# A hybrid DiT layer: shared scan chunks, lasting bias tables and shared value blocks in the stage of scan and attention

## The chip, the cores and the metric

The kernel runs on one core of a Trainium2 chip. The metric is device time in microseconds for one execution. The kernel before took 1521.46 us, the median of three runs (1518.48 to 1524.15).

The core has a matrix engine (PE, with its weight loads PEld), a vector engine (DVE), a scalar engine (ACT), GpSimd (POOL) and SyncE (SP), each with its own instruction stream that it works off in order, and 16 DMA engines that move data between HBM and the on-chip memories. In this kernel SP issues nearly all transfers, one after the other.

## The reference

One layer of a backbone over 1024 latent tokens and 256 context tokens of width 1024. After adaptive norm and one input projection, the columns split into two groups: a gated DeltaNet (four heads of 128, a scan over the sequence in both directions, the context first) and a neighbourhood attention (eight heads of 64, a window of 8 rows by 16 columns on a grid of 16 by 64, with a learned bias and all context keys in one softmax). Both go through one output projection, then a SwiGLU feed-forward network.

```python
px = modulate(rms_norm(x, norm1_w[i]), sh1, sc1) @ w_in[i]
pc = modulate(rms_norm(ctx, norm1_w[i]), csh1, csc1) @ w_in[i]
dn_c, s_ctx_f, s_ctx_b = gated_deltanet(pc[..., :DN_IN], ..., s_zero, s_zero)
dn_x, _, _ = gated_deltanet(px[..., :DN_IN], ..., s_ctx_f, s_ctx_b)
na_x = neighborhood_attention(qx, kx, vx, kc, vc, na_rpb[i], rows)
x = x + g1 * (jnp.concatenate([dn_x, na_x], axis=-1) @ w_out[i])
x = x + g2 * swiglu(modulate(rms_norm(x, norm2_w[i]), sh2, sc2), w_ffn_in[i], w_ffn_out[i])
...
# neighborhood_attention, for the row block r
s_win = jnp.einsum("bnqhd,binchd->bhnqic", q_r, k_r) + bias
s_win = jnp.where(col_valid[:, :, None, :], s_win, -jnp.inf)
s_ctx = jnp.einsum("bnqhd,bkhd->bhnqk", q_r, k_ctx)
p = jax.nn.softmax(jnp.concatenate([s_win.reshape(...), s_ctx], axis=-1), axis=-1)
o = einsum(p_win, v_r) + einsum(p[..., n_win:], v_ctx)
...
# the scan, for each chunk
v_new = u_i - w_i @ S
o_i = (q_i * exp(gam_i)) @ S + qk_i @ v_new
S = S * exp(g_last) + k_dec.T @ v_new
```

The chunks are a way to compute the scan: the kernel uses chunks of 128 tokens, ten in all, of which the first two are the context.

## The kernel before

The kernel has stages in a row: adaptive-norm modulation, input projection, convolution and the preparation of the chunks, then the stage that the change touches, in which the scan and the attention run beside each other (about 552 to 780 us of the profile), then the output projection w_out (from 780 us) and the feed-forward network to the end. Intermediate results lie in HBM between stages.

**The scan.** The loop at L1306 makes ten steps. In step i the forward direction works on chunk ORDER[0][i] (0, 1, 2, ... 9) and the backward one on ORDER[1][i] (1, 0, 9, 8, ... 2). `load(d, c)` at L269 issues the transfers for direction d and chunk c one step ahead: kT, v, y, kt, and for the latent chunks also qT and at, each 128 x 512 floats (256 KB). kT, kt, v and qT depend on the chunk alone; y and at on the direction too. Each tile has three buffers, except that the first step's tiles (`own`) lie in a pool of their own, `begins`, which is closed at step 1 and makes room for the output accumulator oacc. `scan` (L1186) computes one step of one direction in generator pieces; its state S is a new tile `s0` or `s1` in each step. `finish` (L1246) normalises and gates a chunk that both directions have passed, and writes the operands gah and gal of the output projection.

**The attention.** 32 "pairs" follow one another: four pairs of heads, two halves of the rows (`half`), four blocks of columns (`cb`). `pair` (L322) computes the scores of two heads into PSUM (`sc`), adds the bias table in a DVE instruction that also takes the row maximum (L342, out in bt), takes the exponential on ACT in place (L344), normalises on DVE in place (L346), transposes bt on PE (L104, called from L353), copies to pt on ACT (L355) and multiplies with the values vw and vc. The bias tables are tiles bt of 128 x 640 floats in five buffers, two for each pair: `biases` (L301) clears the 256 context columns on POOL (L305) and loads 128 x 384 (L306, 192 KB) for every pair. There are three cases of column blocks (CASE = 0, 1, 1, 2), so that blocks 1 and 2 have equal tables. `values` (L310) loads three of the four groups of rows of a column block (192 KB) for every pair; the two halves of a block share two of them.

**The order.** `beside(PACE)` (PACE = 0.72) advances the attention by so many pieces for each piece of the scan. From the program so written, a scheduler makes each engine's own order, with priorities by program order; on SP all loads stand in one queue, so that a load which must wait for its buffer holds up all loads behind it.

**Towards w_out.** `two_blocks` (L1279) multiplies the attention's half of the first two w_out blocks during the last step and takes its weight pieces from the scan's buffers. After the stage, w_out's weights are loaded to wraw (L217) and split to whi on ACT (L218) and wlo on DVE (L220); the products with gah and gal follow (sc<-gah,whi). Next to it stand the first loads of the feed-forward network's weights, wq<-w_gu (L1393), split to uhi on ACT (L1421) and ulo on DVE (L1422).

Of the kernel before, what the change touches and what calls it, by code (L numbers as in the profile page):

```python
# [9 lines left out]
F32 = mybir.dt.float32  # L10
# [44 lines left out]
AT = (0, 128)  # L55
CTX = {256: slice(0, 256), 0: slice(384, 640)}
PACE = 0.72
ORDER = [list(range(NCH)), [1, 0] + list(range(9, 1, -1))]

# [30 lines left out]
def hybrid(ctx, tc, a, dbg):  # L90
# [174 lines left out]
    ready = {}  # L265
    begins = ExitStack()

    def load(d, c, own=None):

        kT, kt, y, v = (own.tile([128, 4, 128], F32, name=n, tag=f"{n}{d}") if own else  # L270
                        (scan_v if n == "v" else scan_in).tile([128, 4, 128], F32, name=n, tag=n, bufs=3)
                        for n in ("kT", "kt", "y", "v"))
        sp.dma_start(kT, kT_d[:, :, c * 128:(c + 1) * 128])
        sp.dma_start(fl(v), v_d[c * 128:(c + 1) * 128])
        sp.dma_start(y, y_d[d, c])
        sp.dma_start(fl(kt), k_d[c * 128:(c + 1) * 128])
        qT = at = None
        if c >= 2:
            qT, at = (scan_in.tile([128, 4, 128], F32, name=n, tag=n) for n in ("qT", "at"))
            sp.dma_start(qT, qT_d[:, :, (c - 2) * 128:(c - 1) * 128])  # L280
            sp.dma_start(at, at_d[d, c - 2])
        ready[d, c] = kT, qT, kt, v, y, at
# [5 lines left out]
    def attention(nw):  # L288
# [10 lines left out]

        def biases(hp, half, cb):  # L300

            out = []
            for u, w0 in enumerate(WIN):
                bt = nw.tile([128, 640], F32, name="bt", tag="bt", bufs=5)
                pool.memset(bt[:, CTX[w0]], 0.0)  # L305
                sp.dma_start(bt[:, w0:w0 + 384], a["rpb"][2 * hp + u, half, CASE[cb]])  # L306
                out.append(bt)
            return out

        def values(hp, half, cb):  # L310
            vw = nw.tile([128, 3, 128], F32, name="vw", tag="vw", bufs=3)
            sp.dma_start(vw, vw_d[:, cb, half:half + 3, hp * 128:hp * 128 + 128])
            return vw
# [9 lines left out]
        def pair(heads, bts, vw, vc, half, cb, out):  # L323

            r0 = 4 * half
            mx = nw.tile([128, 2, 4], F32, name="mx", tag="mx", bufs=3)
            for u, (head, w0, bt) in enumerate(zip(heads, WIN, bts)):
# [14 lines left out]
                dve.tensor_tensor_reduce(bt, sc, bt, 1.0, -3.0e38, OP.add, OP.max, m[:, 0:1])  # L342
                dve.tensor_scalar(m[:, 1:2], m[:, 0:1], -1.0, None, op0=OP.mult)
                act.activation(bt, bt, AF.Exp, bias=m[:, 1:2], accum_out=m[:, 2:3])  # L344
# [32 lines left out]
        for n, (hp, half, cb) in enumerate(order):  # L377
            if half == 1 and cb in (0, 2) and hp + 1 < NAH // 2:
                heads.setdefault(hp + 1, []).append(load(2 * hp + 2 + cb // 2))
                if cb == 0:  # L380
                    vcs[hp + 1] = context(hp + 1)
# [1455 lines left out]
```

## Time and profile before

| what | us |
|---|---|
| median of the three timed runs | 1521.46 |
| profiled execution, its own time | 1521.66 |
| its span | 1519.9 |
| PE busy in the span | 1455.5 |
| DVE, ACT, POOL busy | 1010.1, 703.1, 183.3 |
| DMA moved in the whole span | 276.28 MB |

The mean granted clock of PE is 0.990 in this execution. The page gives the busy time of each engine, the span in 40 slices, the DMA queues, the chain of work that ended last and the costliest groups of instructions. In the names `out<-in` of an instruction L100 is the helper that issues matmuls and L104 the one that issues transposes, so the tiles tell which is which: `sc<-cst,bt` is a transpose of the softmax, `sc<-kh,qs` a score, `ps<-vk,kt` a product of the scan. SPq is SP's issue of a transfer. A bracket behind a row of a timeline gives the idle time of the engine before the instruction and what ended it.

The chain of work that ended last doesn't reach back before 706 us in this trace, so the stage is read from its waits and timelines.

### The profile page before, as it was taken

The page shows a single profiled execution, that of the slowest core. Times are in us where ns is not written, and L with a number is a line of the kernel's source. Part 1 is how long each engine was busy: PE and PEld are TensorE (multiplying, and loading weights), DVE is VectorE, ACT ScalarE, POOL GpSimd, SP SyncE. Part 2 cuts the span into 40 slices and gives each one's busy share as a digit, 9 for nine tenths or more (in the row PEclk, how much of TensorE's full clock was granted, in tenths as well). Part 3 has the DMA queues.
Part 4 walks back from the last instruction along what each step waited for, and adds up shares of the span by engine and source line. Part 5 has one row for each costly group of instructions (what it writes and reads, how often), then busy time and mean ns, then how long its engine had stood idle before and what let it go on. Part 6 is the DMA issues. An engine that isn't in the chain of part 4 may idle for free.

```text
span 1519.9 us, 23452 instructions
## 1 busy us (share of the span) xinstructions
PE 1455.5 (96%) x8365; PEld 1208.0 (79%) x8365; DVE 1010.1 (66%) x1908; ACT 703.1 (46%) x1379; POOL 183.3 (12%) x251
## 2 busy tenths in 40 slices
PE   6999998899999998999898999999999999999998
PEld 3789787678877777888787888788888888888887
DVE  4787579455677436779977398766665556699652
ACT  5443461674366545656733284333333334354441
POOL 0154500343134300000100000000000000000000
PEclk9999999999999999999999999999999999999999
DMA  9377133565477798999529415333333335798752
GB/s 368 113 229 238 54 94 122 198 170 176 135 214 251 223 289 239 284 269 274 178 76 322 139 35 183 122 105 103 104 102 101 105 104 172 259 366 284 235 153 83
DMA packets 209829, 276.28 MB, mean 182 GB/s; under 512 B 15968, under 2 KB 116912, under 8 KB 208688
## 3 DMA queue, kind: packets, MB, share of 16 engines
q1 hardware_dynamic: 208992, 274.41, 56.3%
q8 instruction: 66, 1.08, 0.3%
q14 instruction: 51, 0.42, 0.1%
q10 hardware_dynamic: 720, 0.37, 0.1%
HBM read 209.93 MB, written 68.98 MB: 184 GB/s over the span
## 4 chain that ended last, share of the span: by engine, by line
PE 45%; DVE 4%; DMA 2%; ACT 1%; issue 1%; SPq 0%; DVEq 0%; ACTq 0%
PE ps L100 42%; PE sc L100 2%; DMA wad<-wa 1%; PE sc L104 1%; DVE x L1591 1%; DVE ulo L1422 1%; DVE acc L254 0%; DMA wraw<-w_out 0%; DVE x L1567 0%; DVE bt L342 0%; DVE lT L1562 0%; DVE x L1470 0%; ACT x L1571 0%; DVE lB L1575 0%; DMA f_d<-g 0%
## 5 line engine op out<-in xcount | busy, mean ns | idle before, releaser
L100 PE MATMUL ps<-hT,uhi 128*128 128x512 f32 x496 | 146.9, 390 | 1.5 <-DVE e L1712 1.4
L100 PE MATMUL ps<-lT,uhi 128*128 128x512 f32 x496 | 146.5, 390 | 0.0
L100 PE MATMUL ps<-hT,ulo 128*128 128x512 f32 x496 | 146.3, 390 | 0.0
L100 PE MATMUL blk<-hh,whi 128*128 128x512 f32 (+1 forms) x456 | 138.8, 397 | 1.9 <-ACT hh L724 1.5
L100 PE MATMUL blk<-hh,wlo 128*128 128x512 f32 (+1 forms) x456 | 130.0, 378 | 0.0
L100 PE MATMUL ps<-hB,uhi 128*128 128x512 f32 x436 | 129.3, 390 | 0.0
L100 PE MATMUL blk<-hl,whi 128*128 128x512 f32 (+1 forms) x456 | 129.2, 377 | 0.0
L100 PE MATMUL ps<-lB,uhi 128*128 128x512 f32 x436 | 128.9, 390 | 0.0
L100 PE MATMUL ps<-hB,ulo 128*128 128x512 f32 x436 | 128.8, 390 | 0.0
L1421 ACT CAST uhi<-ws 128x512 fp32r<-128x512 f32 x91 | 54.7, 622 | 144.8 <-PE ps L100 81.8
L1421 ACT CAST uhi<-wq 128x512 fp32r<-128x512 f32 x101 | 60.3, 621 | 131.3 <-PE ps L100 70.2
L1422 DVE TENSOR_TENSOR ulo<-wq,uhi 128x512 fp32r<-128x512 f32 x101 | 67.2, 688 | 64.8 <-ACT uhi L1421 35.6
L100 PEld LDWEIGHTS ps<-hT,uhi 128*128 128x128 f32 x496 | 93.0, 188 | 21.3 <-ACT uhi L1421 1.7
L100 PEld LDWEIGHTS ps<-lT,uhi 128*128 128x128 f32 x496 | 93.1, 188 | 19.7 <-DVE lT L1575 0.4
L100 PEld LDWEIGHTS ps<-hT,ulo 128*128 128x128 f32 x496 | 93.2, 188 | 19.3
L100 PEld LDWEIGHTS ps<-hB,uhi 128*128 128x128 f32 x436 | 81.9, 188 | 17.4 <-issue 0.5
L100 PEld LDWEIGHTS ps<-lB,uhi 128*128 128x128 f32 x436 | 81.8, 188 | 17.2 <-DVE lB L1575 0.3
L100 PEld LDWEIGHTS ps<-hB,ulo 128*128 128x128 f32 x436 | 81.9, 188 | 16.9
L100 PEld LDWEIGHTS blk<-hh,wlo 128*128 128x128 f32 x456 | 80.7, 191 | 17.8 <-issue 2.5
L100 PEld LDWEIGHTS blk<-hl,whi 128*128 128x128 f32 x456 | 81.0, 190 | 15.2
L100 PEld LDWEIGHTS blk<-hh,whi 128*128 128x128 f32 x456 | 77.5, 192 | 19.1 <-ACT hh L724 3.2
L1422 DVE TENSOR_TENSOR ulo<-ws,uhi 128x512 fp32r<-128x512 f32 x91 | 60.7, 686 | 36.0 <-ACT uhi L1421 27.9
(337 smaller groups left out, 3051.1 us busy)
## 6 DMA issues: line engine op xcount, KB each, us to landing
wq<-w_fo SPq DMA_DIRECT2D x99, 256.0 KB
wq<-w_gu SPq DMA_DIRECT2D x88, 256.0 KB
wad<-wa SPq DMA_DIRECT2D x64, 256.0 KB
bt<-rpb SPq DMA_DIRECT2D x64, 192.0 KB
t_d<-g SPq DMA_DIRECT2D x22, 512.0 KB
fr<-t_d SPq DMA_DIRECT2D x44, 256.0 KB
f_d<-g SPq DMA_DIRECT2D x33, 256.0 KB
fr<-f_d SPq DMA_DIRECT2D x33, 256.0 KB
```

The lines of the kernel that those rows point to most:

```text
L100: i = nc.tensor.matmul(*args, **kw)
L104: i = nc.tensor.transpose(*args, **kw)
L1421: act.copy(hi, self.raw[key])
L1422: dve.tensor_tensor(lo, self.raw[key], hi.bitcast(F32), OP.subtract)
L1591: dve.tensor_tensor(B[at][:, k], B[x][:, k], B.get(y, B["B11"])[:, k], OP.subtract)
```

## The change

- **Chunks.** TWICE holds the chunks that both directions use in two neighbouring steps, with the roles swapped: 0, 1, 5 and 6. Their kT, v, kt and qT are loaded for the direction that comes first and kept for the other (`chunks`). y and at are loaded as before. The pool of the first step's tiles is now closed at step 2.
- **Tables.** Two lasting sets of two tables are cleared once. A set is loaded only when the pair of heads, the half or the case changes. The order of the pairs within a pair of heads becomes TILES, so that equal tables and equal column blocks follow one another: six loads of a set for eight pairs.
- **Values.** A column block is loaded with all four groups of rows and used for both halves.
- **Softmax.** It is computed in tiles of its own, ex, in four buffers, and not in place in the table.
- **State.** The scan's state is updated in place.
- **Room.** The tile sq has the shape of one head, 128 x 128, and one weight piece of `two_blocks` comes from the buffers of v and not from the attention's pool.

```diff
...
 AT = (0, 128)
+TILES = ((0, 0), (0, 1), (1, 1), (2, 1), (2, 0), (1, 0), (3, 0), (3, 1))
 CTX = {256: slice(0, 256), 0: slice(384, 640)}
...
 ORDER = [list(range(NCH)), [1, 0] + list(range(9, 1, -1))]
+TWICE = {c for i in range(NCH - 1) for c in ORDER[0][i:i + 2] if set(ORDER[0][i:i + 2]) == set(ORDER[1][i:i + 2])}
...
     fl = lambda x: x.rearrange("p a b -> p (a b)")
-    ready = {}
+    ready, chunks = {}, {}
     begins = ExitStack()
...
-        kT, kt, y, v = (own.tile([128, 4, 128], F32, name=n, tag=f"{n}{d}") if own else
-                        (scan_v if n == "v" else scan_in).tile([128, 4, 128], F32, name=n, tag=n, bufs=3)
-                        for n in ("kT", "kt", "y", "v"))
-        sp.dma_start(kT, kT_d[:, :, c * 128:(c + 1) * 128])
-        sp.dma_start(fl(v), v_d[c * 128:(c + 1) * 128])
+        def tile(n):
+            if own:
+                return own.tile([128, 4, 128], F32, name=n, tag=f"{n}{d}")
+            return (scan_v if n == "v" else scan_in).tile([128, 4, 128], F32, name=n, tag=n, bufs=3)
+
+        old = chunks.pop(c, None)
+        kT, qT, kt, v = old or (tile("kT"), tile("qT") if c >= 2 else None, tile("kt"), tile("v"))
+        if not old:
+            sp.dma_start(kT, kT_d[:, :, c * 128:(c + 1) * 128])
+            sp.dma_start(fl(v), v_d[c * 128:(c + 1) * 128])
+        y = tile("y")
         sp.dma_start(y, y_d[d, c])
-        sp.dma_start(fl(kt), k_d[c * 128:(c + 1) * 128])
-        qT = at = None
+        if not old:
+            sp.dma_start(fl(kt), k_d[c * 128:(c + 1) * 128])
+        at = None
         if c >= 2:
-            qT, at = (scan_in.tile([128, 4, 128], F32, name=n, tag=n) for n in ("qT", "at"))
-            sp.dma_start(qT, qT_d[:, :, (c - 2) * 128:(c - 1) * 128])
+            if not old:
+                sp.dma_start(qT, qT_d[:, :, (c - 2) * 128:(c - 1) * 128])
+            at = tile("at")
             sp.dma_start(at, at_d[d, c - 2])
+        if not old and c in TWICE:
+            chunks[c] = kT, qT, kt, v
         ready[d, c] = kT, qT, kt, v, y, at
...
+        lasting_bt = [[nw.tile([128, 640], F32, name=f"bt{u}{i}", tag=f"bt{u}{i}", bufs=1) for u in range(2)]
+                      for i in range(2)]
+        for two in lasting_bt:
+            for w0, bt in zip(WIN, two):
+                pool.memset(bt[:, CTX[w0]], 0.0)
+        tables, blocks = [None, 0], {}
+
         def biases(hp, half, cb):
...
-            out = []
-            for u, w0 in enumerate(WIN):
-                bt = nw.tile([128, 640], F32, name="bt", tag="bt", bufs=5)
-                pool.memset(bt[:, CTX[w0]], 0.0)
-                sp.dma_start(bt[:, w0:w0 + 384], a["rpb"][2 * hp + u, half, CASE[cb]])
-                out.append(bt)
-            return out
+            key = hp, half, CASE[cb]
+            if tables[0] != key:
+                out = lasting_bt[tables[1] % 2]
+                for u, w0 in enumerate(WIN):
+                    sp.dma_start(out[u][:, w0:w0 + 384], a["rpb"][2 * hp + u, half, CASE[cb]])
+                tables[:] = key, tables[1] + 1
+            return lasting_bt[(tables[1] - 1) % 2]
...
         def values(hp, half, cb):
-            vw = nw.tile([128, 3, 128], F32, name="vw", tag="vw", bufs=3)
-            sp.dma_start(vw, vw_d[:, cb, half:half + 3, hp * 128:hp * 128 + 128])
-            return vw
+            if (hp, cb) not in blocks:
+                vw = nw.tile([128, 4, 128], F32, name="vw", tag="vw", bufs=3)
+                sp.dma_start(vw, vw_d[:, cb, :, hp * 128:hp * 128 + 128])
+                blocks[hp, cb] = vw
+            return blocks[hp, cb][:, half:half + 3]
...
-            r0 = 4 * half
+            r0, exs = 4 * half, []
             mx = nw.tile([128, 2, 4], F32, name="mx", tag="mx", bufs=3)
...
                 m = mx[:, u]
-                dve.tensor_tensor_reduce(bt, sc, bt, 1.0, -3.0e38, OP.add, OP.max, m[:, 0:1])
+                ex = nw.tile([128, 640], F32, name="ex", tag="ex", bufs=4)
+                dve.tensor_tensor_reduce(ex, sc, bt, 1.0, -3.0e38, OP.add, OP.max, m[:, 0:1])
                 dve.tensor_scalar(m[:, 1:2], m[:, 0:1], -1.0, None, op0=OP.mult)
-                act.activation(bt, bt, AF.Exp, bias=m[:, 1:2], accum_out=m[:, 2:3])
+                act.activation(ex, ex, AF.Exp, bias=m[:, 1:2], accum_out=m[:, 2:3])
                 dve.reciprocal(m[:, 3:4], m[:, 2:3])
-                dve.tensor_scalar(bt, bt, m[:, 3:4], None, op0=OP.mult)
+                dve.tensor_scalar(ex, ex, m[:, 3:4], None, op0=OP.mult)
+                exs.append(ex)
             yield 1
             pts = []
-            for u, bt in enumerate(bts):
+            for u, ex in enumerate(exs):
                 held = slot()
...
                 for j in range(5):
-                    pe.transpose(sc[:, j * 128:(j + 1) * 128], bt[:, j * 128:(j + 1) * 128], ident)
+                    pe.transpose(sc[:, j * 128:(j + 1) * 128], ex[:, j * 128:(j + 1) * 128], ident)
                 pt = nw.tile([128, 640], F32, name="pt", tag="pt", bufs=3)
...
-        order = [(hp, half, cb) for hp in range(NAH // 2) for half in range(2) for cb in range(4)]
+        order = [(hp, half, cb) for hp in range(NAH // 2) for cb, half in TILES]
         heads = {0: [load(0), load(1)]}
...
         for n, (hp, half, cb) in enumerate(order):
-            if half == 1 and cb in (0, 2) and hp + 1 < NAH // 2:
-                heads.setdefault(hp + 1, []).append(load(2 * hp + 2 + cb // 2))
-                if cb == 0:
+            at = n % len(TILES)
+            if at in (4, 6) and hp + 1 < NAH // 2:
+                heads.setdefault(hp + 1, []).append(load(2 * hp + at // 2))
+                if at == 4:
                     vcs[hp + 1] = context(hp + 1)
...
             s = S[d]
+            if s is None:
+                S[d] = work("s%d" % d, 1)
             sc = lambda t, h: t[:, d, c, h:h + 1]
...
                     pe.matmul(p[:, hs[h]], kt[:, h], vk[:, h], start=True, stop=True)
-                sn = work("s%d" % d)
                 for h in range(4):
                     if s is None:
-                        act.copy(sn[:, h], p[:, hs[h]])
+                        act.copy(S[d][:, h], p[:, hs[h]])
                     else:
-                        dve.scalar_tensor_tensor(sn[:, h], s[:, h], sc(ET, h), p[:, hs[h]],
+                        dve.scalar_tensor_tensor(s[:, h], s[:, h], sc(ET, h), p[:, hs[h]],
                                                  op0=OP.mult, op1=OP.add)
-                S[d] = sn
             yield 1
...
             o = oacc[:, c - 2]
-            z, sq = work("z"), work("sq", 1)
+            z = work("z")
+            sq = sw.tile([128, 128], F32, name="sq", tag="sq", bufs=1)
             sp.dma_start(z, zT_d[:, :, (c - 2) * 128:(c - 1) * 128])
...
             for h in range(4):
-                act.activation(sq[:, h], o[:, h], AF.Square, accum_out=r[:, h:h + 1])
+                act.activation(sq, o[:, h], AF.Square, accum_out=r[:, h:h + 1])
             t = sw.tile([128, 3, 4], F32, name="nwt", tag="nwt")
...
                 hi = piece(F32R)
-                lo = piece(F32R) if b == 0 else fw.tile([128, 4, 128], F32R, name="ew", tag="ew", bufs=1)
+                lo = piece(F32R) if b == 0 else scan_v.tile([128, 4, 128], F32R, name="ew", tag="v", bufs=3)
                 act.copy(hi, r)
...
         for i in range(NCH):
-            if i == 1:
+            if i == 2:
                 begins.close()
...
```

The number of instructions on PE (7469), DVE (1910) and ACT (1290) in the program is the same before and after; POOL has 196 rather than 256. The orders of the engines move at three places of interest.

SP in the first steps of the scan (bt and vw are the attention's loads, kT, y, v and kt those of scan step 2, zT_d a store of the stage before). Before:

```order
L306 DMA bt<-rpb 128x384 x2
L273 DMA kT<-kT_d 128x4x128
L275 DMA y<-y_d 128x512
L460 DMA zT_d<-zt 128x1024
L276 DMA kt<-k_d 128x512
L273 DMA kT<-kT_d 128x4x128
L275 DMA y<-y_d 128x512
L274 DMA v<-v_d 128x512 x2
L276 DMA kt<-k_d 128x512
L312 DMA vw<-vw_d 128x3x128
L306 DMA bt<-rpb 128x384
L312 DMA vw<-vw_d 128x3x128
```

After, where bt_4672 to bt_4675 are the four lasting tables:

```order
L325 DMA bt_4674<-rpb 128x384
L325 DMA bt_4675<-rpb 128x384
L332 DMA vw<-vw_d 128x4x128
L283 DMA y<-y_d 128x512
L484 DMA zT_d<-zt 128x1024
L283 DMA y<-y_d 128x512
L280 DMA kT<-kT_d 128x4x128
L283 DMA y<-y_d 128x512
L325 DMA bt_4672<-rpb 128x384
L325 DMA bt_4673<-rpb 128x384
L281 DMA v<-v_d 128x512
L285 DMA kt<-k_d 128x512
```

Both directions' second steps now bring only y, and the third set of tables follows the second after six other transfers, where before there were ten ahead of the third pair's first table, and its second came later still.

SP at the end of the scan (bt the last tables, z the gate of the last chunks, wraw and x the output projection's weights and input, wq the feed-forward network's weights, wad those of the modulation). Before:

```order
L306 DMA bt<-rpb 128x384
L1249 DMA z<-zT_d 128x4x128 x2
L217 DMA wraw<-w_out 128x4x128 x2
L1487 DMA x_8245<-xcT 128x1024 x2
L217 DMA wraw<-w_out 128x8x128
L1393 DMA wq<-w_gu 128x512 x5
L1498 DMA x_d<-x_8245 128x1024
L1393 DMA wq<-w_gu 128x512 x3
L233 DMA wad<-wa 128x512 x4
```

After:

```order
L325 DMA bt_4675<-rpb 128x384
L1274 DMA z<-zT_d 128x4x128 x2
L1418 DMA wq<-w_gu 128x512 x2
L219 DMA wraw<-w_out 128x4x128 x2
L1512 DMA x_8097<-xcT 128x1024 x2
L219 DMA wraw<-w_out 128x8x128
L1418 DMA wq<-w_gu 128x512 x5
L1523 DMA x_d<-x_8097 128x1024
L1418 DMA wq<-w_gu 128x512
L235 DMA wad<-wa 128x512 x4
```

Two of the loads of wq have moved ahead of the first two loads of wraw. Their buffers lie where the constants for the transposes (cst) were, so the first of them waits for the last transpose of `finish`.

ACT at the same place (gah is the last operand that `finish` writes, whi the split weights of w_out, uhi those of the feed-forward network). Before:

```order
L1267 CAST gah<-z 128x4x128 x2
L218 CAST whi<-wraw 128x512 x2
L218 CAST whi<-wraw 128x1024
L1421 CAST uhi<-wq 128x512
L1482 ACTIVATE acc<-x_8245 128x512
```

After:

```order
L1292 CAST gah<-z 128x4x128 x2
L1446 CAST uhi<-wq 128x512 x2
L220 CAST whi<-wraw 128x512 x2
L220 CAST whi<-wraw 128x1024
L1446 CAST uhi<-wq 128x512
```

The casts of the two weights wq now stand ahead of those of w_out, and on DVE the two ulo that belong to them ahead of the first wlo.

## The prediction

> **What bounds the kernel now.** I read the profile from the outside in: the page's busy times, busy time by stretch for the stage that the change touches, the waits of that stage by group, and the timelines of the instants at which TensorE (PE) stood still.
>
> ```profile
> span 1519.9 us, 23452 instructions
> PE 1455.5 (96%) x8365; PEld 1208.0 (79%) x8365; DVE 1010.1 (66%) x1908; ACT 703.1 (46%) x1379; POOL 183.3 (12%) x251
> ```
>
> PE is busy 1455.5 of 1519.9 us, so 64.4 us of idle PE is all that any edit off PE can win, apart from a change of PE's clock. The changed code runs from about 552 to 780 us. The busy time there (columns: stretch, length, then PE, PEld, DVE, ACT, POOL, granted clock, DMA share, GB/s):
>
> ```profile
> 575.00:600.00 25.00, 22.16 (x206) 19.93 (x206) 16.79 (x57) 15.64 (x41) 2.28 (x7) 0.93 0.81 233
> ...
> 650.00:675.00 25.00, 22.78 (x211) 20.88 (x208) 16.99 (x55) 13.59 (x38) 2.21 (x6) 0.93 0.92 244
> ...
> 725.00:750.00 25.00, 23.36 (x234) 20.15 (x233) 24.16 (x93) 16.93 (x42) 3.65 (x9) 1.00 0.68 200
> ...
> sum 228.00, PE 210.23 PEld 184.00 DVE 182.15 ACT 143.78 POOL 21.55; mean PE 21.02 PEld 18.40 DVE 18.21 ACT 14.38 POOL 2.15
> ```
>
> In these 228 us PE idles 228.00 − 210.23 = 17.8 us. The DMA engines are 81 to 92% busy in the first two stretches and DVE only 67%; later it is DVE that has no room (24.16 of 25 us). So a change that moves fewer bytes can act on the first half of the stage. How bytes reach PE is seen in the waits of the stage (waiter <- releaser: us in all, times, the longest):
>
> ```profile
> PE sc L104 <- DVE mx L342: 8.2, 8, 2.1
> ...
> PE sc L100 <- ACT pt L355: 3.8, 7, 1.1
> ...
> DVE bt L342 <- DMA bt<-rpb: 11.6, 5, 4.1
> ...
> POOL bt L305 <- PE sc L104: 94.8, 31, 11.5
> ...
> SPq L306 <- PE sc L104: 22.8, 23, 3.2
> ```
>
> PE has no group here that waits for a scan operand by DMA. The one transfer that arrives late is the bias table (bt<-rpb, L306): DVE waits for it 11.6 us, and PE then for DVE. Its issue on SP waits for the transposes (L104) of an older pair, because the same buffer held that pair's softmax. The instants, on PE and then on DVE (start, length, instruction, idle before it and its releaser):
>
> ```profile
> 573.86 0.76 PE L104 MATMUL sc<-cst,bt 128*128 128x128 f32 x5 [1.55 <-DVE mx L342]
> ...
> 595.33 0.88 PE L104 MATMUL sc<-cst,bt 128*128 128x128 f32 x5 [2.14 <-DVE mx L342]
> ...
> 619.54 0.77 PE L104 MATMUL sc<-cst,bt 128*128 128x128 f32 x5 [1.03 <-DVE mx L342]
> ...
> 663.13 0.66 PE L104 MATMUL sc<-cst,bt 128*128 128x128 f32 x4 [2.06 <-DVE mx L342]
> ...
> 694.61 0.27 PE L100 MATMUL sc<-kh,qs 128*128 128x256 f16 x1 [0.53 <-DVE mx L342]
> ```
>
> ```profile
> 572.97 0.82 DVE L342 CUSTOM_DVE_ANT_0 bt<-sc,bt 128x640 f32<-128x640 f32 x1 [2.15 <-DMA bt<-rpb]
> ...
> 594.44 0.82 DVE L342 CUSTOM_DVE_ANT_0 bt<-sc,bt 128x640 f32<-128x640 f32 x1 [4.09 <-DMA bt<-rpb]
> ...
> 618.65 0.82 DVE L342 CUSTOM_DVE_ANT_0 bt<-sc,bt 128x640 f32<-128x640 f32 x1 [2.01 <-PE sc L104]
> ...
> 662.24 0.82 DVE L342 CUSTOM_DVE_ANT_0 bt<-sc,bt 128x640 f32<-128x640 f32 x1 [3.97 <-DMA bt<-rpb]
> ...
> 693.73 0.82 DVE L342 CUSTOM_DVE_ANT_0 bt<-sc,bt 128x640 f32<-128x640 f32 x1 [0.88 <-DMA bt<-rpb]
> ```
>
> Four PE gaps (573.86, 595.33, 663.13, 694.61) end 0.88 or 0.89 us after a DVE max-reduce that waited for a table: 1.55 + 2.14 + 2.06 + 0.53 = 6.28 us. The fifth, 1.03 us, has the same shape, but there DVE is put down to PE.
>
> **The clock behind two of them.** The two long gaps cost more than their length:
>
> ```profile
> 595.00:598.00 3.00, 2.67 (x15) 2.62 (x16) 2.27 (x7) 1.51 (x3) 0.31 (x1) 0.64 0.54 132
> 598.00:601.00 3.00, 3.00 (x27) 2.71 (x26) 2.47 (x9) 0.92 (x2) 0.00 (x0) 0.79 0.48 153
> ...
> 664.00:667.00 3.00, 3.00 (x17) 3.00 (x16) 2.39 (x8) 0.92 (x2) 0.00 (x0) 0.52 0.75 180
> 667.00:670.00 3.00, 3.00 (x30) 2.82 (x31) 1.80 (x6) 2.17 (x4) 0.97 (x2) 0.91 0.69 212
> ```
>
> ```profile
> 574.46 1.06 PE L100 MATMUL ps<-vk,kt 128*128 128x128 f32 x8
> ...
> 596.21 1.91 PE L100 MATMUL ps<-vk,kt 128*128 128x128 f32 x8
> ```
>
> Behind the gap of 2.14 us the granted clock is 0.64 and 0.79 for three us each, behind that of 2.06 us 0.52 and 0.91, and PE is busy nearly throughout. The same eight matmuls take 1.91 us there and 1.06 us behind the gap of 1.55 us. Lost: 3 × (0.36 + 0.21) = 1.71 us, and 3 × (0.48 + 0.09) = 1.71 us, 3.42 together. The two gaps of 1.55 and 1.03 us show no such loss.
>
> The Trainium skill, "TensorE: Matmul & The Clock Gate", section "What's actually happening", says that the clock halves after an idle window of about 3.4 us, in windows that run freely. By that rule gaps of 2.1 us should leave the clock alone, and removing them would win their length only; that is the second rival below. The trace disagrees (0.64 and 0.52 behind 2.14 and 2.06 us), and the rows decide.
>
> **The change, part by part.**
>
> ```profile
> DMA packets 55622, 53.48 MB, mean 251 GB/s; under 512 B 3760, under 2 KB 44080, under 8 KB 55594
> ```
>
> *Bytes.* Tables: 64 loads of 128x384 floats (0.197 MB) become 48, 3.1 MB less. Values: 32 of 0.197 MB become 16 of 0.262 MB, 2.1 MB less. Chunks 0, 1, 5 and 6 are loaded once for both directions: 3 or 4 tensors each, 14 loads of 0.262 MB, 3.7 MB less. That is 8.9 of the 53.48 MB of the view for 552 to 765 us, and 46 issues on SP. PE waits for none of these directly, so chunks and values are worth nothing by themselves; they thin the queue in front of the tables.
>
> *Tables.* Two lasting sets, reloaded only when the case changes, and softmax in tiles of its own. A table's load now waits only for the max-reduce that last read its set, no longer for softmax, transposes and a memset. The four delays at DVE are 0.88 to 4.09 us. Between a max-reduce and the end of the same pair's transposes lie the exponential, the normalising and the transposes themselves, so the load is released earlier by at least these three (0.55 us and more for the normalising alone, by the row of L346 below), SP no longer stands still at it (22.8 us in 23 waits), and a quarter of the loads is gone. I take the four gaps as removed, −6.28, and the clock with them, −3.42. Bounds: nothing, where SP still comes late, and −6.28 − 3.42 − 1.03 = −10.7 where the fifth goes too. I leave the fifth in, as its row names PE. What is late next: the transposes after DVE's max-reduce, which DVE, 67% busy in these stretches, has room to hide.
>
> *Memsets and softmax tiles.*
>
> ```profile
> L346 DVE TENSOR_SCALAR bt<-bt,mx x64: 543/548/572, 558.9 to 772.0; 128x640 f32<-128x640 f32 x64
> L305 POOL MEMSET bt<- x59: 310/311/673, 560.4 to 762.5; 128x256 f32 x59
> ```
>
> 64 memsets become 4: 60 × 0.31 = 18.6 us off POOL, which is busy 21.55 of 228 us and is waited for only ahead of a table; no term of its own. The new tiles (ex, four buffers) are written when the transposes of two pairs earlier are done, which stand ahead of the present scores in PE's order: nothing either way, at worst one wait as long as the longest for ACT's pt, 1.1 us.
>
> *State in place, the small sq tile, oacc a step later.* The write of the state follows reads that PE does earlier in its own order; the sq tile is written by ACT alone. Nothing either way; bounded by one such wait, 1.1 us. Where a scan load must wait for a chunk held over two steps, all that SP has queued behind it waits too; that is the third rival.
>
> *The start of w_out.* This is the new cost. In the new order two FFN weights (wq) stand ahead of the first w_out weights on SP, and their casts ahead of whi on ACT. Now:
>
> ```profile
> 790.68 0.38 SPq L217 DMA_DIRECT2D wraw<-w_out  x1
> ...
> 793.01 0.56 SPq L217 DMA_DIRECT2D wraw<-w_out  x1
> ```
>
> ```profile
> 790.80 0.62 ACT L218 CAST whi<-wraw 128x512 fp32r<-128x512 f32 x1
> 793.62 0.62 ACT L218 CAST whi<-wraw 128x512 fp32r<-128x512 f32 x1 [2.20 <-DMA wraw<-w_out]
> 800.07 1.05 ACT L218 CAST whi<-wraw 128x1024 fp32r<-128x1024 f32 x1 [5.83 <-DMA wraw<-w_out]
> ```
>
> ```profile
> 788.19 1.03 PE L104 MATMUL ps<-cst,oacc 128*128 128x128 f32 x8
> ...
> 791.84 0.63 PE L100 MATMUL sc<-gah,whi 128*128 128x512 f32 x2
> ...
> 818.00 1.19 PE L100 MATMUL ps<-gah,whi 128*128 128x512 f32 x2 [4.20 <-DVE x L1470]
> ```
>
> ```profile
> 802.30 1.28 DVE L1422 TENSOR_TENSOR ulo<-wq,uhi 128x512 fp32r<-128x512 f32 x2
> ```
>
> The first w_out weights were there before they were needed (cast at 790.80, no wait). Afterwards SP reaches them behind wq, whose buffer is free when the last transposes end, 788.19 + 1.03 = 789.22; three issues of 0.4 to 0.6 us put the w_out issue at about 790.6. From issue to cast took 793.62 − 790.68 = 2.94 us on a quiet queue and 800.07 − 793.01 = 7.06 behind other loads. So the cast starts at 793.5 to 797.7, where it was 790.80: 2.7 to 6.9 us later, and PE with it, since 791.84 followed the cast at once. An idle of 2.7 us is longer than 2.06, so 1.71 of clock comes on top. Coming back: two ulo (1.28 us) and 0.52 MB of wq no longer stand between the next blocks, which shortens the gap of 4.20 us before 818.00 by 1.28 to about 3.4 us (0.52 MB at the view's mean of 251 GB/s adds 2.1); cut to under 2 us, that gap would lose a clock loss of its own. Bounds: 2.7 + 1.71 − 3.4 − 1.71 = −0.7 and 6.9 + 1.71 − 1.28 = +7.3. I take the quiet row, since at 790 us only z and two wq are on the way, and the middle of the return: 2.7 + 1.71 − 2.3 = +2.1.
>
> **The sum**, against the profiled execution's own 1521.66 us (span 1519.9; the median of the three timed runs is 1521.46, so nothing needs correcting): 1521.66 − 6.28 − 3.42 + 2.1 = 1514.1. A measurement of this kernel can tell about 0.5% (7.6 us) from no change; 1514.1 lies almost on that line.
>
> **The rivals.**
> - *More than the four gaps.* With 46 issues less on SP the 1.03 us goes as well, some of ACT's 3.8 us, and w_out starts nearly free: 1521.66 − 10.7 − 1 + 0 = 1510. For it: DMA is up to 92% busy. Against it: ACT's and DVE's late waits have no DMA in them. 22%.
> - *The clock stays out of it.* If the slow clock comes from something else than these gaps, such as the thin work around them, only lengths count: 1521.66 − 6.28 + (2.7 − 2.3) = 1515.8. For it: only two cases carry the argument. Against: clock and gap go together in both, and in none of the shorter gaps. 15%. (By the rule of the Trainium skill, "TensorE: Matmul & The Clock Gate", section "What's actually happening", this case would be the outcome.)
> - *SP blocks on a scan load (slower).* Chunks 5 and 6 occupy two of three buffers for two steps; the load of the step after must wait, and the tables behind it on SP come late. A late table as at 595.33 costs 2.14 + 1.71 = 3.85 us. Two such take back 7.7 of the 9.7; with three or four and w_out at +7.3, 1521.66 − 9.7 + 3.5 × 3.85 + 7.3 = 1532.7, with w_out at +2.1 1527.5. It decides from the point where tables are issued later ahead of their max-reduce than before (SP's wait before L306 was 22.8 us in all). For it: SP is one queue in order. Against: 46 fewer issues. 8%.
> - *The bytes were hidden anyway.* The gaps close, but DVE, 24.16 of 25 us busy from 725 us, makes PE wait later for what PE gained: 1519 to 1522. For it: the late stage is DVE's. Against: DVE idles 46 of 228 us and could start its late work sooner. 20%.
>
> **How the numbers follow.** Forecast 35% (1511 to 1517 on its own), then 22, 15, 8, 20. The range reaches from inside the first rival (1507 to 1512 on its own) past the fourth: 1508 to 1523, and leaves out some 5% below and 8% above. Faster by over 0.5%, under 1513.9: all of the first rival and half of the forecast's own range, 0.41; slower by over 0.5%, above 1529: half of the third rival and a little for what isn't named, 0.05; the rest 0.54.
>
> **What will show it.** In the waits of the stage, DVE's group "max-reduce <- DMA of a table" should fall from 11.6 us to under 3, and no 3-us stretch between 575 and 700 should show a clock under 0.9. PE's idle in the stage should fall from 17.8 to about 11.5. At the start of w_out PE should show a new gap of 2.7 to 6.9 us that ends on ACT's whi, with a low clock behind it; the gap near 818 should be shorter. The prediction is wrong if table waits remain with fewer bytes, if new gaps appear from 700 us on, or if w_out starts without a gap.

## The result and the profile after

The changed kernel takes 1513.57 us, the median of seven runs (1507.78 to 1516.54), beside 1523.79 us for the kernel before (seven runs, 1518.48 to 1524.25). The ratio is 0.9936 with a 95% interval of 0.9915 to 0.9958. The profiled execution took 1511.45 us. The page's busy times of the changed kernel:

```profile
span 1509.7 us, 23086 instructions
...
PE 1453.5 (96%) x8365; PEld 1205.7 (80%) x8365; DVE 1007.9 (67%) x1908; ACT 704.7 (47%) x1379; POOL 164.6 (11%) x191
```

PE does the same work; what shrank is its idle time and its slow clock. The three stretches shown of before, and the sum over 552 to 780 us (columns as before: stretch, length, PE, PEld, DVE, ACT, POOL, granted clock, DMA share, GB/s):

```profile
575.00:600.00 25.00, 24.84 (x249) 22.16 (x248) 20.91 (x70) 16.07 (x42) 0.00 (x0) 1.00 1.03 298
...
650.00:675.00 25.00, 24.93 (x249) 22.34 (x248) 21.27 (x68) 16.25 (x44) 0.00 (x0) 1.00 0.92 257
...
725.00:750.00 25.00, 22.99 (x224) 19.18 (x222) 23.44 (x97) 18.30 (x53) 2.57 (x2) 1.00 0.42 128
...
sum 228.00, PE 218.69 PEld 191.25 DVE 190.29 ACT 150.61 POOL 2.57; mean PE 21.87 PEld 19.12 DVE 19.03 ACT 15.06 POOL 0.26
```

PE idles 9.3 us in these 228 us, where it was 17.8. The stretches with a clock of 0.93 are at 1.00. The late stretch, where DVE has little room, is as it was (22.99 us of PE work against 23.36). In the waits of the stage the group of DVE that waits for a table is gone, and the two groups that were PE's largest (8.2 us behind DVE's max-reduce, 3.8 us behind ACT's pt) are now small:

```profile
PE sc L102 <- ACT pt L378: 2.0, 4, 1.0
...
PE sc L106 <- DVE mx L364: 1.1, 3, 0.5
```

The start of w_out shows the new cost, on PE, then SP, ACT and the clock (L102 and L106 are the helpers that were L100 and L104):

```profile
775.82 1.03 PE L106 MATMUL ps<-cst,oacc 128*128 128x128 f32 x8
...
783.14 1.22 PE L102 MATMUL sc<-gah,whi 128*128 128x512 f32 x2 [3.54 <-ACT whi L220]
...
809.65 0.70 PE L102 MATMUL ps<-gah,whi 128*128 128x512 f32 x2 [1.90 <-ACT ws L1500]
```

```profile
776.88 0.83 SPq L1418 DMA_DIRECT2D wq<-w_gu  x2
777.77 0.97 SPq L219 DMA_DIRECT2D wraw<-w_out  x2
```

```profile
779.59 1.26 ACT L1446 CAST uhi<-wq 128x512 fp32r<-128x512 f32 x2 [1.07 <-DMA wq<-w_gu]
782.47 1.14 ACT L220 CAST whi<-wraw 128x512 fp32r<-128x512 f32 x2 [1.62 <-DMA wraw<-w_out]
```

```profile
783.00:786.00 3.00, 2.86 (x7) 2.28 (x8) 1.29 (x2) 0.61 (x2) 0.00 (x0) 0.50 0.76 288
786.00:789.00 3.00, 3.00 (x9) 2.34 (x8) 0.00 (x0) 0.00 (x0) 0.00 (x0) 0.56 1.07 341
```

SP issues wq as soon as the last transposes end (775.82 + 1.03), w_out behind it at 777.77; ACT has the weights at 782.47; PE has stood for 3.54 us and then runs at half clock for most of 6 us.

To say where the time went, I cut both traces at three marks on PE: the first product of the scan (ps<-v,y), the last transposes of the scan (ps<-cst,oacc) and the first product of the feed-forward network (ps<-hB,uhi). Stage is from the first to the second, w_out from the second to the third. The table holds the experiments too; "table wait" is DVE's wait for a table by DMA between 552 and 780 us.

| run | table wait | stage | w_out | ratio to before (95%) |
|---|---|---|---|---|
| before | 11.6 | 237.0 | 88.6 | 1 |
| changed | none | 222.9 | 91.2 | 0.9936 (0.9915 to 0.9958) |
| e1 old tables | 4.8 | 226.7 | 91.3 | 0.9945 (0.9923 to 0.9967) |
| e2 tables only | 6.5 | 230.2 | 88.5 | 0.9949 (0.9927 to 0.9970) |
| e3 every table | 0.4 | 226.7 | 92.1 | 0.9919 (0.9898 to 0.9941) |
| e4 w_out first | none | 224.5 | 88.8 | 0.9904 (0.9880 to 0.9928) |
| e5 release only | 12.7 | 232.6 | 92.2 | 0.9966 (0.9951 to 0.9980) |
| e6 chunks only | 2.3 | 230.4 | 91.4 | 0.9961 (0.9945 to 0.9977) |
| e7 early third | none | 222.9 | 85.5 | 0.9888 (0.9867 to 0.9909) |
| e9 tables by ACT | 4.1 | 243.3 | 91.2 | 1.0049 (1.0029 to 1.0069) |

For the changed kernel the stage gave 14.1 us and w_out took 2.6. The first product of the scan stands 1.7 us later in this execution (552.90 against 551.18). In the eight experiments on the layer it stands at 550.47 to 551.28, also in e4, whose stage is that of the changed kernel, so I put this down to the execution and not to the change. The rest after w_out is 0.4 us shorter: 1.7 − 14.1 + 2.6 − 0.4 = −10.2 = 1509.7 − 1519.9. Stage and w_out are one profile each, so a difference of one or two us between two of them says little. Between the marks of the stage (before, then changed; columns as above) PE idles 237.01 − 219.24 = 17.8 us and 222.92 − 214.90 = 8.0 us:

```profile
551.18:788.19 237.01, 219.24 (x2044) 191.51 (x2045) 188.14 (x684) 146.35 (x409) 21.55 (x61) 0.99 0.80 229
```

```profile
552.90:775.82 222.92, 214.90 (x2045) 188.30 (x2046) 187.53 (x684) 148.11 (x409) 2.57 (x2) 1.00 0.72 202
```

### The profile page after: what moved, and what is told of

Its sections match the earlier page's. It is cut to its first block, busy times and chain, and to the rows that moved or that the text cites. A ratio compares the mean times of both kernels' runs of the same rounds, so it can differ in the third digit from the quotient of the medians.

```text
span 1509.7 us, 23086 instructions
## 1 busy us (share of the span) xinstructions
PE 1453.5 (96%) x8365; PEld 1205.7 (80%) x8365; DVE 1007.9 (67%) x1908; ACT 704.7 (47%) x1379; POOL 164.6 (11%) x191
## 4 chain that ended last, share of the span: by engine, by line
PE 67%; DVE 8%; DMA 5%; ACT 5%; issue 2%; SPq 1%; POOL 0%; ACTq 0%; DVEq 0%; POOLq 0%
PE ps L102 45%; PE blk L102 10%; PE sc L102 5%; PE pr L102 3%; DMA nv_d<-zt 2%; PE sc L106 2%; PE m L102 1%; DMA wad<-wa 1%; DMA wraw<-w_nqk 1%; DVE acc L256 1%; ACT ex L366 1%; DVE x L1616 1%; DVE cacc L520 1%; SPq L1093 1%; DVE ex L368 0%
## 5 line engine op out<-in xcount | busy, mean ns | idle before, releaser
L102 PE MATMUL ps<-hT,uhi 128*128 128x512 f32 x496 | 146.8, 390 | 0.9 <-DVE e L1737 0.8
L102 PE MATMUL ps<-lT,uhi 128*128 128x512 f32 x496 | 146.4, 389 | 0.0
L102 PE MATMUL ps<-hT,ulo 128*128 128x512 f32 x496 | 146.2, 389 | 0.0
L102 PE MATMUL blk<-hh,whi 128*128 128x512 f32 (+1 forms) x456 | 139.3, 397 | 2.1 <-ACT hh L748 1.8
L102 PE MATMUL blk<-hl,whi 128*128 128x512 f32 (+1 forms) x456 | 130.1, 379 | 0.0
L102 PE MATMUL blk<-hh,wlo 128*128 128x512 f32 (+1 forms) x456 | 129.9, 378 | 0.0
L102 PE MATMUL ps<-hB,uhi 128*128 128x512 f32 x436 | 129.1, 390 | 0.0
L102 PE MATMUL ps<-lB,uhi 128*128 128x512 f32 x436 | 128.9, 389 | 0.0
L102 PE MATMUL ps<-hB,ulo 128*128 128x512 f32 x436 | 128.7, 389 | 0.0
L102 PEld LDWEIGHTS ps<-hT,uhi 128*128 128x128 f32 x496 | 92.9, 188 | 20.7 <-ACT uhi L1446 1.2
L102 PEld LDWEIGHTS ps<-lT,uhi 128*128 128x128 f32 x496 | 93.0, 188 | 19.7 <-DVE lT L1600 0.4
L102 PEld LDWEIGHTS ps<-hT,ulo 128*128 128x128 f32 x496 | 93.1, 188 | 19.4
L102 PEld LDWEIGHTS ps<-hB,uhi 128*128 128x128 f32 x436 | 81.8, 188 | 17.4 <-issue 0.5
L102 PEld LDWEIGHTS ps<-lB,uhi 128*128 128x128 f32 x436 | 81.8, 188 | 17.3 <-DVE lB L1600 0.4
L102 PEld LDWEIGHTS ps<-hB,ulo 128*128 128x128 f32 x436 | 81.8, 188 | 17.0
L102 PEld LDWEIGHTS blk<-hh,wlo 128*128 128x128 f32 x456 | 80.9, 191 | 17.9 <-issue 1.7
L102 PEld LDWEIGHTS blk<-hl,whi 128*128 128x128 f32 x456 | 81.6, 192 | 15.5
L102 PEld LDWEIGHTS blk<-hh,whi 128*128 128x128 f32 x456 | 77.3, 192 | 19.4 <-ACT hh L748 3.7
```

What stands on the lines that cost most here:

```text
L102: i = nc.tensor.matmul(*args, **kw)
```

## The experiments

**e1: the tables undone.** The diff is against the changed kernel, as all diffs below.

```diff
-                ex = nw.tile([128, 640], F32, name="ex", tag="ex", bufs=4)
+                ex = bt
...
+                bt = nw.tile([128, 640], F32, name="bt", tag="bt", bufs=5)
+                pool.memset(bt[:, CTX[w0]], 0.0)
+                sp.dma_start(bt[:, w0:w0 + 384], a["rpb"][2 * hp + u, half, CASE[cb]])
```

> The changed kernel with one part undone: bias tables as before (five buffers, cleared and loaded for every pair, softmax in place); shared chunks and shared value blocks stay, 5.8 MB less than before. Theory A (release): what made tables late is that a table's buffer was held until the transposes; then the late tables come back, DVE's wait for a table by DMA in the stage is 8 us or more, PE idles 15 us or more in 552 to 780 us, and the ratio to the kernel before is 0.997 to 1.003. Theory B (bytes): what made them late is the queue of transfers in front; then 5.8 MB less is most of the cure, DVE waits under 4 us for tables, PE idles under 12 us, and the ratio is 0.994 to 0.996.

DVE's waits for a table are five short ones (total, times, longest), and PE idles 11.2 us in the stage:

```profile
DVE bt L359 <- DMA bt<-rpb: 4.8, 5, 2.2
...
sum 228.00, PE 216.76 PEld 189.44 DVE 190.03 ACT 149.14 POOL 21.40; mean PE 21.68 PEld 18.94 DVE 19.00 ACT 14.91 POOL 2.14
```

Theory B fits in idle time and ratio, with a wait a little over its bound: with tables held as before and the chunks and value blocks loaded less often, more than half of the wait is gone and 10.3 of the stage's 14.1 us. The run also keeps the smaller edits (the order of the pairs, the state in place, the sq tile), whose part in the 10.3 us wasn't tried.

**e2: tables alone.**

```diff
-TWICE = {c for i in range(NCH - 1) for c in ORDER[0][i:i + 2] if set(ORDER[0][i:i + 2]) == set(ORDER[1][i:i + 2])}
+TWICE = set()
...
-            if (hp, cb) not in blocks:
-                vw = nw.tile([128, 4, 128], F32, name="vw", tag="vw", bufs=3)
-                sp.dma_start(vw, vw_d[:, cb, :, hp * 128:hp * 128 + 128])
-                blocks[hp, cb] = vw
-            return blocks[hp, cb][:, half:half + 3]
+            vw = nw.tile([128, 3, 128], F32, name="vw", tag="vw", bufs=3)
+            sp.dma_start(vw, vw_d[:, cb, half:half + 3, hp * 128:hp * 128 + 128])
+            return vw
```

> The changed kernel with chunks loaded for each direction and three row groups of values for every pair again (5.8 MB more); lasting tables and softmax in own tiles stay. Theory A (release): as the changed kernel, DVE waits under 3 us for tables, ratio 0.992 to 0.995. Theory B (bytes): DVE waits 4 to 8 us for tables, ratio 0.997 to 1.000.

Two tables are late, each with a long gap on PE behind it and a slow clock behind that (first the wait, then PE, then the clock):

```profile
DVE ex L362 <- DMA bt<-rpb: 6.5, 2, 3.8
```

```profile
589.48 1.33 PE L106 MATMUL sc<-cst,ex 128*128 128x128 f32 x5 [3.62 <-DVE mx L362]
```

```profile
589.00:592.00 3.00, 2.52 (x12) 2.52 (x13) 2.18 (x8) 1.10 (x2) 0.00 (x0) 0.50 0.90 186
592.00:595.00 3.00, 3.00 (x17) 2.99 (x17) 1.46 (x4) 2.37 (x8) 0.00 (x0) 0.53 0.03 9
```

The wait lies in the span of theory B, the ratio (0.9949) at the edge of theory A's, so the run doesn't decide by its time. But two late tables are left: releasing a table early doesn't suffice where the scan's loads are as many as before.

**e3: a set loaded for every pair.**

```diff
-            if tables[0] != key:
+            if True:
```

> The changed kernel, but a set of tables is loaded for every pair, 64 loads and not 48 (3.1 MB more), still into the two lasting sets and with the softmax in own tiles. Theory A (release): as the changed kernel, ratio 0.992 to 0.995, DVE waits under 3 us for tables. Theory B (bytes and fewer loads): DVE waits 3 to 8 us, ratio 0.995 to 0.998.

The matmuls on PE stand in the same order as in the changed kernel, and the tables are in time:

```profile
DVE ex L364 <- DMA bt<-rpb: 0.4, 1, 0.4
```

So the 16 loads saved by using a table twice bring nothing here that can be measured: 0.9919 with 64 loads, 0.9936 with 48, and the intervals overlap. Most of the 3.8 us by which its stage is longer in the profile lie at one place: the stretch 552 to 575 us had a clock of 0.85 (0.15 × 23 = 3.5 us) behind a gap on PE that ended on ACT's vk, not on a table:

```profile
552.00:575.00 23.00, 19.97 (x166) 17.75 (x165) 13.20 (x44) 15.10 (x44) 0.00 (x0) 0.85 0.85 261
```

```profile
557.34 3.09 PE L102 MATMUL ps<-vk,kt 128*128 128x128 f32 x16 [1.83 <-ACT vk L1244]
```

Set beside e1, which also has 64 table loads and the same chunks and value blocks, e3 shows what the lasting sets and own softmax tiles bring once the other loads are fewer. The wait for tables falls from 4.8 to 0.4 us and the median from 1516.79 us (1513.62 to 1518.22) to 1512.10 us (1510.10 to 1514.48), although the stage is as long in the two profiles.

**e5 and e6: release alone, chunks alone.** e5 is e2 with the edit of e3, so all loads are as many as before and the lasting sets and own softmax tiles remain. e6 is e1 with e2's edit of the values, so the shared chunks remain. Both keep the smaller edits.

> The changed kernel with chunks, values and table loads all as often as before (64 table loads of 0.197 MB, all scan loads for each direction); what stays of the change is that the tables have lasting sets and the softmax its own tiles, so a table's load waits for the max-reduce only. Theory A (release) of the prediction: no late tables, DVE waits under 3 us for tables, ratio to the kernel before 0.992 to 0.995. Theory C, formed after the first four runs: a table is late because SP comes late, behind the row of ten to twelve scan loads of a step; then tables are late in the early steps as in the run with lasting tables alone, DVE waits 6 us or more, PE shows two or more gaps over 2 us behind them, ratio 0.995 to 0.999.

> The changed kernel with tables and values as before; shared chunks stay (14 fewer loads, 3.7 MB). Theory C (SP's row of scan loads): this is the part that counts, DVE waits under 6 us for tables, no PE gap over 2 us between 570 and 700 us, ratio 0.993 to 0.997. Rival D (bytes, wherever they are saved): 3.7 of 5.8 MB give less than the run with old tables (0.9945), DVE waits 6 to 9 us, ratio 0.997 to 0.999.

```profile
DVE ex L362 <- DMA bt<-rpb: 12.7, 7, 5.1
```

```profile
DVE bt L357 <- DMA bt<-rpb: 2.3, 2, 1.7
```

The first line is of e5, the second of e6. With release alone DVE waits for tables as long as before (12.7 us, before 11.6); with 14 loads of chunks fewer it waits 2.3 us. In e5 only one PE gap over 2 us followed a table, of 3.19 us at 659 us, not two or more. In e6 no PE gap over 2 us stands between 570 and 700 us, as theory C had it. The ratio of each lies in the range of theory C, and rival D's wait of 6 to 9 us didn't come. But in ratio the two runs are alike, so the times don't show that the chunks are worth more than the release: each gives between a half and two thirds of the gain of the whole change. And part of the gain isn't late tables at all (the stage of e5 is 4.4 us shorter than before at the same table wait); which edit or which order makes it, wasn't tried.

**e9: the tables issued by ACT.** e5 with one word changed: is it the place in SP's row, or the amount?

```diff
-                    sp.dma_start(out[u][:, w0:w0 + 384], a["rpb"][2 * hp + u, half, CASE[cb]])
+                    act.dma_start(out[u][:, w0:w0 + 384], a["rpb"][2 * hp + u, half, CASE[cb]])
```

> The run with release only (all transfers as often as before), but the 64 table loads are issued by ACT and no longer stand in SP's row behind the scan loads; the bytes are the same. Theory C (SP comes late to the tables): DVE waits under 4 us for tables where it waited 12.7, and the ratio falls from 0.9966 to 0.995 or less, unless ACT's own issues and waits eat it (64 issues of 0.3 to 0.5 us, some 25 us of an engine that is 62% busy in the stage). Theory C' (bytes: the DMA engines are full in the first 150 us of the stage, 94.6% of the hardware queue's time there before): tables stay late, DVE waits 6 us or more, ratio 0.996 to 1.001.

```profile
ACT na L388 <- DMA bt<-rpb: 11.0, 2, 7.3
...
DVE ex L362 <- DMA bt<-rpb: 4.1, 2, 2.3
```

It is slower than before (1.0049), which neither theory forecast, though theory C had named ACT's own issues as what could eat the gain. DVE waits 4.1 us for tables where it waited 12.7, but now ACT stands still. Ahead of its longest wait in the lines above stand four issues of tables in ACT's own order:

```profile
624.88 4.71 ACTq L325 DMA_DIRECT2D bt<-rpb  x4
629.68 0.27 ACT L388 CAST na<-sc 128x128 fp32r<-128x128 f32 x1 [7.32 <-DMA bt<-rpb]
```

Between 552 and 780 us nine waits of ACT, 33.7 us in all, end on some transfer by the trace; in e5 none does. The wait moved and grew; the run leaves open how much of a table's delay is SP's row and how much is full DMA engines. That the wait for tables falls with fewer loads is shown by e1 and e6.

**e4: w_out ahead of the feed-forward weights.** The first wq loads are pinned behind the two loads of the input x on SP, which follow the first two of w_out; everything else is the scheduler's choice (`behind` puts one instruction after another in the order of their engine, without a wait).

```diff
+                ins = sp.dma_start(t, a["w_fo"][f[1], i, h] if isinstance(f, tuple) else a["w_gu"][f, i, h])
+                if pins:
+                    behind(ins, pins[0])
...
+            pins[:] = [sp.dma_start(x2[:, b], a["xcT"][b, :, CT:])]
```

> The changed kernel with one order pinned on SP: the first FFN weights (wq) behind the first two loads of w_out, as in the kernel before. My theory: the w_out weights wait for nothing late (the last reader of their buffer ends on POOL at 743.5 us), so PE starts gah with whi without the gap of 3.54 us and without the low clock behind it; 4 to 5 us of gain at that place, of which the gap before the third block (1.90 us now, 4.20 before) may take back up to 2.3 and its clock 1.7; ratio to the kernel before 0.990 to 0.992. Rival: the later blocks are paced by the weights' own arrival, so the gap moves there and the ratio stays at 0.993 to 0.994.

PE starts almost without a gap, and the gap ahead of the fourth block of w_out is back:

```profile
779.79 0.74 PE L102 MATMUL sc<-gah,whi 128*128 128x512 f32 x2 [0.30 <-ACT whi L220]
...
805.69 1.19 PE L102 MATMUL ps<-gah,whi 128*128 128x512 f32 x2 [3.85 <-DVE x L1504]
```

From 91.2 us w_out falls to 88.8, about the 88.6 of the kernel before. Both theories had a part: the first gap went, 2 of its 3.5 us came back at the second. That the new order costs time is likely and not certain. Of the seven profiles with wq ahead of w_out six show 91.2 to 92.2 us; the seventh is e2 with 88.5, where the first gap is nearly as long but the clock stayed at 1.00:

```profile
787.76 0.74 PE L102 MATMUL sc<-gah,whi 128*128 128x512 f32 x2 [3.34 <-ACT whi L220]
...
787.76:790.76 3.00, 3.00 (x13) 2.46 (x14) 1.32 (x2) 0.54 (x1) 0.00 (x0) 1.00 0.75 270
```

So part of the price is the clock behind the gap, which not every execution pays, and the interval of e4's ratio overlaps that of the changed kernel.

**e7: the fourth block's weights a store earlier.** On top of e4:

```diff
+            if b:
+                early = load_w(a["w_out"][3], lo_engine=dve)
             for p, s in zip(outs, HV):
                 add(b, s, p)
             sp.dma_start(x2_d[b], x2[:, b])
...
-            w, nxt = nxt, load_w(a["w_out"][b + 1], lo_engine=dve)
+            w, nxt = nxt, early if b == 2 else load_w(a["w_out"][b + 1], lo_engine=dve)
```

> The run with w_out first, and the weights of w_out's fourth block loaded ahead of the second block's store, which waits for DVE (SP issues them before it and not after). If the gap of 3.85 us ahead of that block comes from the late load, it shrinks to about 1.9 us (then the eviction of the block before still sets it) and the low clock behind it goes: 2 to 4 us less than with w_out first, ratio 0.987 to 0.990. Rival: the eviction and DVE's order set the gap anyway; the gap stays over 3 us and the ratio at 0.990.

```profile
801.81 0.70 PE L102 MATMUL ps<-gah,whi 128*128 128x512 f32 x2 [2.03 <-DVE x L1504]
```

The gap is 2.03 us instead of 3.85, the first matmuls behind it take 0.70 us and not 1.19, so the clock stayed up, and w_out takes 85.5 us. The rival, in which the gap stays over 3 us, is out. At 1507.17 us (1502.26 to 1511.17) and a ratio of 0.9888 this version beats both kernels.

**e8: the clock by itself.** Not the layer: 96 bursts of 64 dense matmuls (128 rows of the trace), with a chain of DVE instructions ahead of each.

```diff
+        for _ in range(64):
+            pe.matmul(p, x[:, 0:128], t, start=True, stop=True)
+        dve.tensor_tensor(t, p, x[:, 256:384], OP.mult)
+        for _ in range(n):
+            dve.tensor_scalar(t, t, 1.0e-2, None, op0=OP.mult)
```

> Not the layer: 96 bursts of 64 matmuls (128x128x128, float32), dense, each burst ahead of a chain of 1 to 20 DVE instructions of 128x128 on which the next burst waits; the output is the input copied. It measures what an idle gap after dense work does to the granted clock. Theory G (the gap itself, as the prediction had it): gaps over 2 us are followed by matmuls at about half speed for some 3 us, gaps under 1.5 us never, and between 1.5 and 2.1 us some are, by where they fall. Rival T (the thin work around them): after dense work gaps under 3.4 us leave the clock alone.

Five bursts of its timeline on PE (start, length of the burst, gap ahead of it):

```profile
81.60 16.19 PE L111 MATMUL p<-t,x 128*128 128x128 f32 x128 [2.21 <-DVE t L115]
...
102.09 16.74 PE L111 MATMUL p<-t,x 128*128 128x128 f32 x128 [4.31 <-DVE t L115]
120.53 14.56 PE L111 MATMUL p<-t,x 128*128 128x128 f32 x128 [1.69 <-DVE t L115]
...
213.37 14.56 PE L111 MATMUL p<-t,x 128*128 128x128 f32 x128 [1.96 <-DVE t L115]
231.45 14.56 PE L111 MATMUL p<-t,x 128*128 128x128 f32 x128 [3.52 <-DVE t L115]
```

Counted over all bursts: behind the 32 gaps of 0.38 to 1.69 us every burst takes 14.56 us. Behind 1.95 us seven of eight take 16.2 us, behind 2.21 and 2.48 us all sixteen 16.0 to 16.2, behind 2.73 us six of seven, behind 3.52 us seven of eight, and behind 5.35 us the bursts take up to 17.3 us. So theory G holds but for a few bursts: the gap itself does it, after dense work too, from just under 2 us on, and whether it does is no matter of length alone.

## Why the prediction was right or wrong

The forecast was 1514.1 us, 7.6 us under the profiled execution of before. Measured were 1513.57 us and, by the ratio, 0.64% or 9.8 us of 1523.79. It was inside the forecast's own range, and the case was the one expected; part of the way there was not. That the time came within 0.5 us of the forecast is in part luck: the stage gave 4.4 us more than the sum had, and of these 1.7 went with the later start of the scan and 0.5 at w_out, while the kernel before now measured 2.1 us above the execution that the forecast starts from.

- **That late tables were the loss of the stage** was right for the larger part, and so were the gaps to go: none of the four is left, and the fifth (1.03 us), which I had left in, went too. The stage gave 14.1 us for the 9.7 of the sum. Counted between the marks, PE idles 9.75 us less, where the sum had 6.28; the fifth gap and 1.8 us less behind ACT's pt are in this, as the first rival had it. PE is also busy 4.3 us less, of which 3.4 are the clock; the remaining 0.9 us I can't place.
- **Why the tables would come in time** was wrong in what it put first. The step read: "A table's load now waits only for the max-reduce that last read its set, no longer for softmax, transposes and a memset." That is what the change does, but it doesn't cure the delay by itself: with it alone DVE waits for tables 12.7 us (e5). And the step on bytes, "chunks and values are worth nothing by themselves; they thin the queue in front of the tables", had the right mechanism in its second half and priced it at nothing: chunks alone bring the wait to 2.3 us (e6), chunks and values without the release the stage to 226.7 us (e1). Only then does the release take the rest of the wait (4.8 to 0.4 us, from e1 to e3). I had read SP's wait for the transposes (22.8 us in 23 waits) as the cause, and "SP no longer stands still at it" as the cure. In the changed kernel SP still stands there, for DVE's max-reduce, and no table is late:

```profile
SPq L325 <- DVE mx L364: 22.2, 13, 7.4
```

  What I should have set against it is what SP issued just ahead of a late table. In the kernel before, ahead of the tables that DVE had at 594.44 us, these are the first and the last of ten scan loads in a row, and then the tables:

```profile
581.72 0.56 SPq L273 DMA_DIRECT2D kT<-kT_d  x1
...
587.00 0.52 SPq L280 DMA_DIRECT2D qT<-qT_d  x1
587.88 1.00 SPq L306 DMA_DIRECT2D bt<-rpb  x2
```

  Ahead of these tables SP paused only 0.36 us (587.52 to 587.88). The ten loads are 2.62 MB, some 11 us of transfer at the 233 GB/s of that stretch (an estimate), and SP issued them in 5.8 us.

- **The clock term** was right in kind and size: 3.42 us for two gaps, and 16.19 − 14.56 = 1.63 us for each such gap in e8, where I had 1.71. The rival in which only lengths count is out. The rule of the Trainium skill, "TensorE: Matmul & The Clock Gate", section "What's actually happening", that it takes an idle window of about 3.4 us, is not borne out as a bound: gaps of 2.21 and 2.48 us sufficed 16 times of 16 in e8. Its windows that run freely do fit what was seen, that equal gaps of 1.95 us cost a clock loss once and not another time.
- **The start of w_out** came out as worked out: idle 3.54 us in the range of 2.7 to 6.9, clock of 0.50 and 0.56 behind it, the next gap 1.90 for 4.20 us and without a clock loss. The clock cost 3 × (0.50 + 0.44) = 2.8 us where the sum had 1.71. Net +2.6 us for the +2.1 of the sum, in this execution; e2, with the same order, lost nothing here. e4, which puts the order back, takes 2.4 of them away.
- **The other rivals.** SP blocking on a chunk that is held for two steps was not seen: no table is late. That the late stage would take back the gain was wrong too: PE's 22.99 us of 25 there is about what it was.

## What to carry to other kernels

An operand that arrives late on a shared queue can come in time once the transfers in front of it are fewer, also ones that nobody waits for; freeing its buffer earlier cut the wait here only beside that. Look at what the queue issued in the microseconds before, not only at what the late load itself waited for. An idle gap of 2 us on PE can cost nearly as much again in clock (1.63 us in e8, in most bursts but not in all), so gaps of that length can be worth more than they look. After a change, look at what the scheduler put in front of the next stage's first load; pinning that one order, and one load ahead of one store, gave a further 0.5%.

## What the runs showed of the hardware that was not expected

The same gap of 1.95 us, ahead of the first softmax transposes, left the clock alone in the changed kernel and halved it in e4. The first row and the first window are of the changed kernel, the second ones of e4:

```profile
561.31 0.73 PE L106 MATMUL sc<-cst,ex 128*128 128x128 f32 x5 [1.95 <-DVE ex L368]
```

```profile
562.00:565.00 3.00, 3.00 (x29) 2.93 (x29) 1.53 (x6) 3.00 (x10) 0.00 (x0) 1.00 0.93 298
```

```profile
559.65 1.26 PE L106 MATMUL sc<-cst,ex 128*128 128x128 f32 x5 [1.95 <-DVE ex L368]
```

```profile
560.00:563.00 3.00, 3.00 (x16) 3.00 (x15) 0.48 (x2) 3.00 (x12) 0.00 (x0) 0.50 1.09 338
```

In 3 us PE did 29 instructions there and 16 here. That is some 1.5 us between two executions of the same instructions, and several such gaps may be why the runs of one kernel spread here by 6 to 9 us; this was not shown. In the kernel before, too, a gap of 1.95 us at this place (559.59 us) left the clock at 1.00.
